# Two layers of attention on one core: the second layer's key and value weights split during the output projection, other accumulator banks for its first gate block, the first modulation ranked ahead of all, small loads issued by GpSimd

## Chip, cores and metric

The kernel runs on one core of one Trainium2 chip. Its time is device time in microseconds; the smaller the better. A profiled execution gives a trace; TensorE (PE in the rows), VectorE (DVE), ScalarE (ACT), GpSimd (POOL) and SyncE (SP, which here only issues loads and stores) each work through a queue of their own in order, and wait for each other by semaphores. The granted TensorE clock was 1.0 in the profiled execution.

## The reference

A trunk of two layers on 256 tokens of width 1024, in float32. Each layer makes a modulation from the condition `c` (shift, scale and gate), normalises `x`, modulates it, mixes tokens by attention and adds the gated result to `x`:

```python
cond = jax.nn.silu(c)
for i in range(DEPTH):
    shift, scale, gate = jnp.split(cond @ ada_w[i] + ada_b[i], 3, axis=-1)
    h = rms_norm(x, norm_g[i]) * (1 + scale[:, None, :]) + shift[:, None, :]
    y = nsa_mixer(h, ...) if i == 0 else moba_mixer(h, ...)
    x = x + gate[:, None, :] * y
```

Both mixers project `h` by a wide weight into queries (16 heads of 64), keys and values (4 heads) and a gate `z`, normalise queries and keys per head, rotate a quarter of each head by position, take softmax attention, multiply by `silu(z)` and project back by `w_out`. The first layer has three attentions side by side (over 15 compressed blocks, over selected blocks, over a window) and a gate for each. With 256 tokens every block is selected and the window covers all, so each is causal attention over all keys. The second layer has one block of 256 keys, so it is plain causal attention.

## The kernel before

The matrix products run in a reduced-width float format, each weight and activation split into a high part and the remainder (`hi`, `lo`); a product is three matmuls: hi·hi, hi·lo, lo·hi. A weight piece of 256 rows by 512 columns is loaded (`piece`), ScalarE casts it to `hi`, VectorE subtracts to get `lo` (`parts_of`, lines 624 to 631). Tokens come in two blocks of 128, called m = 0 and 1.

The program is first recorded and then ordered by a planner (`Plan`, from line 53). Each recorded operation has a cost from a table, its data dependencies, and a level: FIRST_OF_ALL -2, URGENT -1, CHAIN 0, FILL 1. `issue` walks a modelled clock per engine and gives each engine what can start first, then the lower level, then the earlier recorded one; an operation of a negative level that starts within 250 ns is waited for. So a change of a cost, a level or the order of recording can move any instruction of the whole kernel. Tiles come from tags with a fixed number of buffers: among them `hi` 4, `lo` 4, `raw` 5 (loaded pieces), `n_parts` 2, `qg` 5, and in the accumulator memory `acc` 2 and `ps` 6 banks. An operation whose tile finds no free buffer waits.

Stages that the change touches:

- **Start** (lines 487 to 1108). `c`, `x` and vectors are loaded; the first 128 columns of the modulation (`load_columns`, `ada_ss`) and the first 128 rows of the projection (`load_rows`) come first, so that the projection can begin on a part of the inner dimension; then the rest in stages (`START`). The modulation's result `AB` turns the normalised, transposed input into `HT`, the left operand of the projections. `small_loads` (lines 496 to 500) is a generator: six small loads (positions and five vectors), handed to SP one at a time between the big loads of `load_columns(1)` and `load_rows(1)`. Their reader on TensorE is the product of `ones` with `ROWV` in `tables` (line 1005), after which GpSimd computes rotation tables that are needed at the first key normalisation.
- **First layer's output projection and the next layer's entry** (lines 1364 to 1415). `out_products` runs the two token blocks one behind the other; when block 0 is done, its update of `x`, normalisation, modulation and split into `HT` (`x_part`, `next_h`) run at FIRST_OF_ALL while TensorE does block 1. Before block 1's last part, `first_parts` records the split of the first two of four key/value weight pieces of the second layer into the space of the first layer's keys (`KTF`), free by then. `chunk(m_in, KVB, ...)` then runs block 0 over all four pieces, then block 1.
- **Gate blocks** (`z_blocks`, lines 784 to 804). Each makes 512 columns of `z`, transposed, into two accumulator banks; tanh on ScalarE and a product on VectorE empty them into `zT`. In the second layer both blocks use the two `acc` banks, and their products are the filler beside the attention of `pair_b`.

Of the kernel before, what the change touches and what calls it, by code (L numbers as in the profile page):

```python
# [17 lines left out]
P = 128  # L18
# [34 lines left out]
class Plan:  # L53
# [120 lines left out]
    def _cost(self, engine, method, args, kw, aps):  # L174
        def free(a):
            n = 1
            for _, k in a.ap[1:]:
                n *= k
            return n

        if "dma" in method:
            self.bytes = free(aps[0]) * aps[0].shape[0] * 4
            if aps[1].shape[-1] <= 128 and self.bytes > 1e5:
                self.bytes *= SHORT_ROWS
            if self.bytes <= 1e5:
                self.bytes += SMALL
            return ISSUE if engine == "A" else max(ISSUE, self.bytes / RATE)
        psum = any(str(a.space).endswith("PSUM") for a in aps)
        n = max(free(a) for a in aps)
        if engine == "T":  # L190
            if method == "transpose":
                return 262.0 if aps[1].dtype == F32 else 180.0
            cols = free(aps[2])
            if aps[2].dtype == F32:
                m = free(aps[1])
                if "tile_position" in kw and m <= 64:
                    return max(cols * 4.28 * max(32, m) / P, 60.0)
                return 2 * max(cols * 2.14, 264.0)
            return max(cols * (1.07 if aps[2].dtype == F32R else 1.0), 264.0)
        if engine == "A":  # L200
            return 0.833 * n + (51.0 if psum else 94.0) + 93.0 * sum(isinstance(kw.get(k), bass.AP) for k in ("bias", "scale", "accum_out"))
        if engine == "G":
            return 1.5 * n + 270.0
        if method == "reciprocal":
            return 6.5 * n + 68.0
        fast = not psum and (method == "tensor_copy" or method.startswith("tensor_scalar"))
        pointers = len(aps) - 2 if method.startswith("tensor_scalar") else 0
        return (0.521 if fast else 1.042) * n + 68.0 + 61.0 * pointers
# [22 lines left out]
    def issue(self, opening=()):  # L231
# [51 lines left out]
        while done < len(ops):  # L283
# [57 lines left out]
            clock[e] = end  # L341
            seen = end + self.SEEN[e]
            if "bytes" in op:
                if e == "A":
                    seen = start + (BEHIND if op["level"] > 0 else 2400.0)
                else:
                    wire = max(wire, start + ISSUE + FIRST_BYTE) + op["bytes"] / (EARLY_RATE if start < 5e4 else RATE)
                    seen = wire + (450.0 if start < 5e4 else LANDED)
                    landings.append(seen)
                    if start < DEEP:  # L350
                        clock[e] = max(start + ISSUE, landings[-8] if len(landings) >= 8 else 0.0)
# [49 lines left out]
def kernel(  # L401
# [82 lines left out]
    def row(ap, n):  # L484
        return bass.AP(tensor=ap.tensor, offset=ap.offset, ap=[[n, 1], [1, n]])
# [7 lines left out]
        A.dma_start(R[ROW_B1 - 8:ROW_B1 - 8 + 4, :], rows_of(nsa_cmp_b1, 4))  # L493
        A.dma_start(R[ROW_PE - 8:ROW_PE - 8 + 32, :], rows_of(nsa_cmp_pe, 32))

    def small_loads():
        yield Q.dma_start(PR[:, 0].bitcast(I32), bass.AP(tensor=positions.tensor, offset=positions.offset, ap=[[P, 2], [1, P]]))
        for at, ap, n in ((0, nsa_q_norm, 64), (64, nsa_k_norm, 192), (256, moba_q_norm, 64), (320, moba_k_norm, 64),
                          (384, nsa_gate_b, 48)):
            yield Q.dma_start(ROWV[:, at:at + n], row(ap, n))  # L500

    identF = const.tile([P, P], F32, name="identF")
    make_identity(nc, identF)
# [277 lines left out]
            if count[m] == 8 // KP:  # L781
                done(m, accs[m])

    def z_blocks(w, c0, out):

        accs = [tile_of("acc", 2, S) for _ in range(2)]
        for kp in range(4):
            parts = parts_of(piece(w, kp, (c0, 512)))
            for k in range(KP):
                kt = KP * kp + k  # L790
                for b in range(4):
                    cols = slice(b * P, (b + 1) * P)
                    with plan.at(FILL):
                        for i, (a, part) in enumerate(((0, 0), (0, 1), (1, 0))):
                            T.matmul(accs[b // 2][:, b % 2], parts[part][:, k, cols], HT[:, a, kt, :],
                                     start=(kt == 0 and i == 0 and b % 2 == 0), stop=(kt == 7 and i == 2),
                                     skip_group_check=True)
            if kp < 3:
                yield
        for acc in accs:  # L800
            t, zT = tile_of("y", 2, S), tile_of("zT", 2, S)
            A.activation(t, acc, AF.Tanh, scale=0.5)
            V.scalar_tensor_tensor(zT, t, 1.0, acc, op0=OP.add, op1=OP.mult)
            out += [zT[:, 0], zT[:, 1]]
# [113 lines left out]

    loaded, kv_w = {}, {}

    smalls = small_loads()
    TABLES = 0
    R_AFTER = 0

# [12 lines left out]
    def load_columns(k):  # L937

        pieces = []
        for q in range(2):  # L940
            t = tile_of("early", 2, 4, P)
            pieces.append([t[:, 0], t[:, 1]])
            for s in range(2):
                with plan.at(CHAIN):
                    Q.dma_start(t[:, s], bass.AP(tensor=ada_w.tensor, offset=ada_w.offset + 4 * q * P * 3 * D + s * D + k * P,
                                                 ap=[[3 * D, P], [P * 3 * D, 4], [1, P]]))
                if k:
                    next(smalls, None)
        return pieces

    def load_rows(k):

        a, b = tile_of("early", 1024), tile_of("early", 768)
        rows = slice(k * P, (k + 1) * P)
        with plan.at(CHAIN):
            for c0 in (0, 512):
                Q.dma_start(a[:, c0:c0 + 512], w_in[rows, 1024 + c0:1536 + c0])
            if k:
                next(smalls, None)
            Q.dma_start(b[:, 0:512], w_in[rows, 2048:2560])  # L960
            if k:
                next(smalls, None)
            Q.dma_start(b[:, 512:768], w_in[rows, 0:256])
        return a, b

# [1 line left out]
    lead_s.append(load_columns(1))  # L967
    lead_w.append(load_rows(1))
    xT = [tile_of("n_out", 4, S) for _ in range(2)]
    xs, first_t = [], []  # L970
    RT1 = const.tile([P, ROW_ADA + 16], F32, name="RT1")
    for m in range(2):
        xm, ss = tile_of("n_in", D), tile_of("ss", 16)[:, 0:1]
        xs.append(xm)
        with plan.at(URGENT):
            A.activation(xm, X[:, m, :], AF.Square, accum_out=ss)
            r = rstd_of(ss, 1, 1.0 / D)
        for q in range(2):
            sl = slice(512 * q, 512 * q + 512)
            t = tile_of("ps", 4, P)  # L980
            with plan.at(FILL if q else URGENT):
                if q:
                    A.activation(xm[:, sl], X[:, m, sl], AF.Copy, scale=r)
                else:
                    V.tensor_scalar_mul(xm[:, sl], X[:, m, sl], r)
                with plan.group():
                    for k in range(4):
                        T.transpose(t[:, k, :], xm[:, (4 * q + k) * P:(4 * q + k + 1) * P], identF)
            with plan.at(FILL):
                A.copy(xT[q][:, 1 - q:, m * P:(m + 1) * P], t[:, 1 - q:])  # L990
            if not q:
                first_t.append(t)
        if m == R_AFTER:
            columns(R, 8)
            V.tensor_scalar_add(RT1[:, ROW_ADA + 8:ROW_ADA + 16], RT[:, ROW_ADA + 8:ROW_ADA + 16], 1.0)
# [60 lines left out]
                G.tensor_copy(TC[:, j, m, 0:16], TR[:, kind, m])  # L1056
        return TCS, NBc, TC, TR, TS

    def parts_2d(t, cuts):
        n = t.shape[1]  # L1060
        hi, lo = tile_of("hi", n), tile_of("lo", n)
        for c0, c1 in zip(cuts, cuts[1:] + (n,)):
            with plan.at(FILL):
                A.copy(hi[:, c0:c1], t[:, c0:c1])
                V.tensor_sub(lo[:, c0:c1], t[:, c0:c1], hi[:, c0:c1].bitcast(F32))
        return hi, lo

    for k in range(2):
        with plan.at(URGENT):
            at_once(ada_ss(0, k, 1, lead_s[k]))  # L1070
            for m in range(2):
                toks = slice(m * P, (m + 1) * P)
                src = xT[0][:, k, toks] if k else first_t[m][:, 0]
# [3 lines left out]
                    affine(h, src, 0, k, V)  # L1077
                    V.tensor_sub(HT[:, 1, k, toks], h, HT[:, 0, k, toks].bitcast(F32))
        a, b = lead_w[k]
        w = [(p, sl) for p, cuts in ((parts_2d(a, (0, 512) if not k else (0,)), (0, 512, 1024)), (parts_2d(b, (0,)), (0, 512, 768)))  # L1080
             for sl in (slice(c0, c1) for c0, c1 in zip(cuts, cuts[1:]))]
        for m in range(2):
            for ci, ((hi, lo), sl) in enumerate(w):
# [6 lines left out]
    for at, (what, k0, *rest) in enumerate(START):  # L1090
        load_stage(what, k0, *rest)
        if at == TABLES:
            at_once(smalls)
            TCS, NBc, TC, TR, TS = tables()
        if what == "s":
            nk = rest[0]
# [300 lines left out]
    at_hand = {}  # L1397

    def first_parts():
        for kp in range(2):  # L1400
            at_hand[kp] = parts_of(piece(m_in, kp, *KVB), (KTF[:, 2 * kp], KTF[:, 2 * kp + 1]))

    out_products(w_out, done_a, FINE, first_parts)
    assert not side
# [18 lines left out]
    make_q(raw_q, 4, QT, 2)  # L1423
    side.append(ada_gate(1))
    zT = []
    for c0 in (1536, 2048):
        for _ in z_blocks(m_in, c0, zT):
            beside()

    def pair_b(i):  # L1430
# [61 lines left out]
```

## Time and profile before

| | |
|---|---|
| median of 3 runs | 322.57 us (321.73 to 322.77) |
| profiled execution | 322.3 us, span 320.5 us |
| PE busy | 307.2 us, 96% |
| VectorE busy | 242.1 us, 76% |
| ScalarE busy | 204.9 us, 64% |
| GpSimd busy | 24.8 us, 8% |
| loaded from HBM | 64.36 MB, 204 GB/s over the span |

A timeline row reads: start, duration (us), engine, line, operation, output tile <- input tiles, shape, count of merged instructions, and in brackets the idle time of the engine before it with what ended that time. Nearly all instructions have line 373, where the planner issues them, so they are told apart by tiles. PEld is TensorE's weight load. The ends of matmuls are modelled and overlap the next start; the starts are what counts.

### The profile page before, as it was taken

To read this page: it belongs to the slowest core of one execution; us is meant where nothing else is said; L and a number is where in the kernel's file an instruction comes from. 1 tells how busy PE (TensorE), PEld (TensorE's weight loads), DVE (VectorE), ACT (ScalarE), POOL (GpSimd) and SP (SyncE) were. 2 spreads that over 40 slices of the span, in tenths; PEclk is the share of its full clock that TensorE was granted. 3 is DMA by queue.
4 is the path that set the end of the run, shared out by engine and by line. 5 is a ranking of instruction groups with operands and counts; after the bars stand their busy time and mean duration, and the time that the engine had idled before them with its cause. 6 is when DMAs were issued, how large, how long until landed. Compare 5 with 4: busy or idle time off the path is not lost.

```text
span 320.5 us, 6156 instructions
## 1 busy us (share of the span) xinstructions
PE 307.2 (96%) x2141; PEld 245.3 (77%) x2141; DVE 242.1 (76%) x732; ACT 204.9 (64%) x486; POOL 24.8 (8%) x96
## 2 busy tenths in 40 slices
PE   4899999999999999999999999988999989999995
PEld 4666677777757897768788888856888988886884
DVE  4764375669972999636979877893999999999564
ACT  5635145765735896465899854894676689988320
POOL 6038930000000000000000000000000000000000
PEclk9999999999999999999999999999999999999999
DMA  8999999559799805778074539236589651136302
GB/s 251 319 332 368 367 360 272 159 175 338 265 325 296 292 7 177 235 252 304 24 261 133 190 81 281 105 73 193 167 271 306 183 190 27 54 122 200 127 33 100
DMA packets 43995, 65.81 MB, mean 205 GB/s; under 512 B 4042, under 2 KB 20793, under 8 KB 43964
## 3 DMA queue, kind: packets, MB, share of 16 engines
q1 hardware_dynamic: 43796, 65.36, 63.1%
q8 instruction: 17, 0.28, 0.4%
q14 instruction: 14, 0.11, 0.1%
q10 hardware_dynamic: 168, 0.06, 0.1%
HBM read 64.36 MB, written 1.05 MB: 204 GB/s over the span
## 4 chain that ended last, share of the span: by engine, by line
PE 72%; DVE 12%; DMA 7%; ACT 4%; issue 3%; ACTq 0%; SPq 0%; DVEq 0%
PE ps L373 46%; PE acc L373 26%; DVE lo L373 3%; DVE rs L373 2%; DMA p<-in_nsa_cmp_w_dram 2%; DMA raw<-in_nsa_w_in_dram 2%; DMA y<-in_ada_b_dram 2%; ACT n_out L373 1%; DVE gate L373 1%; DVE n_out L373 1%; DMA early<-in_nsa_w_in_dram 1%; ACT hi L373 1%; ACT HT L373 1%; DVE p L373 1%; DVE ss L373 1%
## 5 line engine op out<-in xcount | busy, mean ns | idle before, releaser
L373 DVE TENSOR_TENSOR lo<-raw,hi 128x1024 fp32r<-128x1024 f32 (+1 forms) x50 | 58.9, 1184 | 21.3 <-ACT hi L373 21.1
L373 ACT CAST hi<-raw 128x1024 fp32r<-128x1024 f32 (+1 forms) x50 | 51.0, 1025 | 34.0 <-PE acc L373 19.7
L373 PE MATMUL acc<-hi,HT 128*128 128x512 f32 (+1 forms) x176 | 54.4, 381 | 2.0 <-ACT HT L373 1.5
L373 PE MATMUL acc<-HT,hi 128*128 128x256 f32 x256 | 49.8, 285 | 1.0 <-DVE zT L373 1.0
L373 ACT ACTIVATE p<-p,tiny 128x128 f32<-128x128 f32 (+1 forms) x96 | 42.9, 454 | 7.5 <-DVE tiny L373 7.4
L373 PEld LDWEIGHTS acc<-HT,hi 128*128 128x128 f32 x256 | 40.1, 188 | 1.8 <-DVE zT L373 1.2
L373 PEld LDWEIGHTS acc<-hi,HT 128*128 128x128 f32 x176 | 32.1, 188 | 10.5 <-issue 2.4
L373 PE MATMUL acc<-HT,lo 128*128 128x256 f32 x128 | 36.8, 288 | 0.0
L373 PE MATMUL acc<-lo,HT 128*128 128x512 f32 (+1 forms) x88 | 33.5, 383 | 1.5 <-DVE lo L373 1.5
L373 DVE CUSTOM_DVE_ANT_0 p<-ps,causal 128x128 f32<-128x128 f32 (+1 forms) x96 | 30.9, 346 | 3.3 <-PE ps L373 3.3
L373 PE MATMUL ps<-hi,HT 128*128 128x512 f32 (+1 forms) x96 | 28.2, 366 | 0.0
L373 PE MATMUL ps<-KTA,qg 128*128 128x256 f32 (+1 forms) x192 | 27.1, 286 | 0.0
L373 ACT COPY pT<-ps 128x384 f32<-128x384 f32 x48 | 21.7, 483 | 5.7 <-PE ps L373 5.6
L373 PEld LDWEIGHTS ps<-KTA,qg 128*128 128x128 f32 x192 | 24.1, 189 | 1.6 <-issue 1.4
L373 PEld LDWEIGHTS acc<-HT,lo 128*128 128x128 f32 x128 | 24.2, 189 | 0.3 <-issue 0.2
L373 PE MATMUL ps<-hi,qg 128*128 128x256 f32 (+1 forms) x96 | 23.7, 320 | 0.0
L373 PE MATMUL acc<-hi,qg 128*128 128x512 f32 x64 | 22.6, 403 | 0.0
L373 PE MATMUL ps<-identF,p 128*128 128x128 f32 x144 | 21.7, 277 | 0.0
L373 PEld LDWEIGHTS acc<-lo,HT 128*128 128x128 f32 x88 | 16.5, 188 | 5.2 <-DVE lo L373 2.8
L373 PEld LDWEIGHTS ps<-hi,HT 128*128 128x128 f32 x96 | 16.8, 188 | 4.5 <-issue 2.5
L373 PE MATMUL ps<-pT,VA 128*64 128x256 f32 (+1 forms) x192 | 19.1, 334 | 0.0
L373 PEld LDWEIGHTS ps<-identF,p 128*128 128x128 f32 x144 | 16.1, 141 | 3.5 <-issue 1.0
(199 smaller groups left out, 565.2 us busy)
## 6 DMA issues: line engine op xcount, KB each, us to landing
raw<-in_ada_w_dram SPq DMA_DIRECT2D x32, 512.0 KB, 4.4
raw<-in_moba_w_in_dram SPq DMA_DIRECT2D x20, 512.0 KB, 4.5
early<-in_ada_w_dram SPq DMA_DIRECT2D x12, 512.0 KB, 9.7
raw<-in_nsa_w_in_dram SPq DMA_DIRECT2D x12, 512.0 KB, 7.3
early<-in_nsa_w_in_dram SPq DMA_DIRECT2D x9, 512.0 KB
p<-in_nsa_cmp_w_dram SPq DMA_DIRECT2D x16, 256.0 KB, 3.7
raw<-in_nsa_w_out_dram SPq DMA_DIRECT2D x8, 512.0 KB, 6.0
raw<-in_moba_w_out_dram SPq DMA_DIRECT2D x8, 512.0 KB, 4.6
```

The source lines that it names most:

```text
L373: r = getattr(self.engines[e], method)(*[self._real(a) for a in args], **{k: self._real(a) for k, a in kw.items()})
```

## The change

Five edits.

1. `first_parts` splits all four key/value pieces of the second layer, the third into two `n_parts` buffers and the fourth into two `qg` buffers.
2. `z_blocks` takes the tag of its accumulators; the second layer's first gate block uses two `ps` banks, the second block `acc` as before.
3. The first modulation step (`ada_ss(0, 0, ...)`) goes from URGENT to FIRST_OF_ALL. The copies of the transposed input out of the accumulator memory, recorded before it until now, are recorded after it and made to depend on its last operation, as are the `lo` subtractions of the first projection piece.
4. The six small loads go from SP to GpSimd's queue, all at FILL level ahead of everything else; the generator and its calls are gone.
5. The planner's cost and landing model: only SP's loads are charged by bytes; a load by GpSimd costs its engine 450 ns and is taken as landed 5.5 us after issue at FILL level, as ScalarE's were.

```diff
@@ Plan._cost
-            return ISSUE if engine == "A" else max(ISSUE, self.bytes / RATE)
+            return max(ISSUE, self.bytes / RATE) if engine == "S" else ISSUE
@@ Plan.issue
-                if e == "A":
+                if e != "S":
                     seen = start + (BEHIND if op["level"] > 0 else 2400.0)
@@
-    def small_loads():
-        yield Q.dma_start(PR[:, 0].bitcast(I32), bass.AP(tensor=positions.tensor, ...))
+    with plan.at(FILL):
+        G.dma_start(PR[:, 0].bitcast(I32), bass.AP(tensor=positions.tensor, ...))
         for at, ap, n in ((0, nsa_q_norm, 64), (64, nsa_k_norm, 192), (256, moba_q_norm, 64), (320, moba_k_norm, 64),
                           (384, nsa_gate_b, 48)):
-            yield Q.dma_start(ROWV[:, at:at + n], row(ap, n))
+            G.dma_start(ROWV[:, at:at + n], row(ap, n))
@@ z_blocks
-    def z_blocks(w, c0, out):
-        accs = [tile_of("acc", 2, S) for _ in range(2)]
+    def z_blocks(w, c0, out, home="acc"):
+        accs = [tile_of(home, 2, S) for _ in range(2)]
@@ start
-            with plan.at(FILL):
-                A.copy(xT[q][:, 1 - q:, m * P:(m + 1) * P], t[:, 1 - q:])
+            evac.append((xT[q][:, 1 - q:, m * P:(m + 1) * P], t[:, 1 - q:]))
...
-    def parts_2d(t, cuts):
+    def parts_2d(t, cuts, after=()):
...
                 A.copy(hi[:, c0:c1], t[:, c0:c1])
-                V.tensor_sub(lo[:, c0:c1], t[:, c0:c1], hi[:, c0:c1].bitcast(F32))
+                with plan.group(after=after):
+                    V.tensor_sub(lo[:, c0:c1], t[:, c0:c1], hi[:, c0:c1].bitcast(F32))
...
     for k in range(2):
+        with plan.at(URGENT if k else FIRST_OF_ALL):
+            at_once(ada_ss(0, k, 1, lead_s[k]))
+        known = [plan.ops[-1]["id"]] if not k else ()
+        if not k:
+            for dst, src in evac:
+                with plan.at(FILL), plan.group(after=known):
+                    A.copy(dst, src)
         with plan.at(URGENT):
-            at_once(ada_ss(0, k, 1, lead_s[k]))
...
-        w = [... parts_2d(a, (0, 512) if not k else (0,)) ...]
+        w = [... parts_2d(a, (0, 512) if not k else (0,), known) ...]
@@ first_parts
-        for kp in range(2):
-            at_hand[kp] = parts_of(piece(m_in, kp, *KVB), (KTF[:, 2 * kp], KTF[:, 2 * kp + 1]))
+        homes = [(KTF[:, 0], KTF[:, 1]), (KTF[:, 2], KTF[:, 3]),
+                 (tile_of("n_parts", KP, 512), tile_of("n_parts", KP, 512)),
+                 (tile_of("qg", KP, 512), tile_of("qg", KP, 512))]
+        for kp in range(4):
+            at_hand[kp] = parts_of(piece(m_in, kp, *KVB), homes[kp])
@@ second layer
-    for c0 in (1536, 2048):
-        for _ in z_blocks(m_in, c0, zT):
+    for c0, home in ((1536, "ps"), (2048, "acc")):
+        for _ in z_blocks(m_in, c0, zT, home):
             beside()
```

More of the change, by code (lines that the diff above doesn't have):

```diff
@@ L494 @@
         A.dma_start(R[ROW_PE - 8:ROW_PE - 8 + 32, :], rows_of(nsa_cmp_pe, 32))
-    def small_loads():
-        yield Q.dma_start(PR[:, 0].bitcast(I32), bass.AP(tensor=positions.tensor, offset=positions.offset, ap=[[P, 2], [1, P]]))
+    with plan.at(FILL):
+        G.dma_start(PR[:, 0].bitcast(I32), bass.AP(tensor=positions.tensor, offset=positions.offset, ap=[[P, 2], [1, P]]))
         for at, ap, n in ((0, nsa_q_norm, 64), (64, nsa_k_norm, 192), (256, moba_q_norm, 64), (320, moba_k_norm, 64),
                           (384, nsa_gate_b, 48)):
-            yield Q.dma_start(ROWV[:, at:at + n], row(ap, n))
+            G.dma_start(ROWV[:, at:at + n], row(ap, n))
     identF = const.tile([P, P], F32, name="identF")
@@ L919 @@
     loaded, kv_w = {}, {}
-    smalls = small_loads()
     TABLES = 0
@@ L946, in load_columns @@
                                                  ap=[[3 * D, P], [P * 3 * D, 4], [1, P]]))
-                if k:
-                    next(smalls, None)
         return pieces
@@ L957, in load_rows @@
                 Q.dma_start(a[:, c0:c0 + 512], w_in[rows, 1024 + c0:1536 + c0])
-            if k:
-                next(smalls, None)
             Q.dma_start(b[:, 0:512], w_in[rows, 2048:2560])
-            if k:
-                next(smalls, None)
             Q.dma_start(b[:, 512:768], w_in[rows, 0:256])
@@ L969 @@
     xT = [tile_of("n_out", 4, S) for _ in range(2)]
-    xs, first_t = [], []
+    xs, first_t, evac = [], [], []
     RT1 = const.tile([P, ROW_ADA + 16], F32, name="RT1")
@@ L1079 @@
         a, b = lead_w[k]
-        w = [(p, sl) for p, cuts in ((parts_2d(a, (0, 512) if not k else (0,)), (0, 512, 1024)), (parts_2d(b, (0,)), (0, 512, 768)))
+        w = [(p, sl) for p, cuts in ((parts_2d(a, (0, 512) if not k else (0,), known), (0, 512, 1024)), (parts_2d(b, (0,)), (0, 512, 768)))
              for sl in (slice(c0, c1) for c0, c1 in zip(cuts, cuts[1:]))]
@@ L1092 @@
         if at == TABLES:
-            at_once(smalls)
             TCS, NBc, TC, TR, TS = tables()
```

## The prediction, made before the result

> **What bounds the kernel now.** I read the page first, then windows of the span, then timelines of the three places that the change touches.
>
> ```profile
> span 320.5 us, 6156 instructions
> PE 307.2 (96%) x2141; PEld 245.3 (77%) x2141; DVE 242.1 (76%) x732; ACT 204.9 (64%) x486; POOL 24.8 (8%) x96
> DMA  8999999559799805778074539236589651136302
> raw<-in_ada_w_dram SPq DMA_DIRECT2D x32, 512.0 KB, 4.4
> ```
>
> TensorE is busy 96% of the span, so all that the change can win is TensorE idle time. The DMA row says that the first seven slices, some 52 us, run at the full rate of the DMA engines. In windows (columns: window, length, busy us and count of PE, PEld, DVE, ACT, POOL, clock, DMA share, GB/s):
>
> ```profile
> 8.00:12.00 4.00, 3.65 (x49) 2.79 (x40) 3.10 (x13) 3.08 (x7) 0.00 (x0) 1.00 1.07 326
> 12.00:16.00 4.00, 3.16 (x27) 2.22 (x27) 2.94 (x7) 2.26 (x5) 0.00 (x0) 1.00 1.12 312
> ```
>
> ```profile
> 230.00:290.00 60.00, 59.03 (x454) 53.42 (x453) 59.32 (x190) 47.66 (x120) 0.00 (x0) 1.00 0.53 173
> ```
>
> So the start has two limits, TensorE and the DMA engines (share 1.07 and 1.12), and the second layer from 230 to 290 has two as well: PE 59.03 and VectorE 59.32 of 60. A gain on PE there counts only if DVE comes forward too.
>
> **Part 1, key and value weights split in the output projection.** Before, two of the four pieces are split ahead, into the free KTA tile; the other two wait for buffers of `hi` and `lo`. The second layer's entry on TensorE:
>
> ```profile
> 207.48 2.96 PE L373 MATMUL acc<-KTA,HT 128*128 128x512 f32 x12
> ...
> 210.28 0.39 PE L373 MATMUL acc<-hi,HT 128*128 128x512 f32 x1
> 211.25 0.51 PE L373 MATMUL acc<-lo,HT 128*128 128x512 f32 x1 [0.57 <-DVE lo L373]
> ...
> 212.29 0.85 PE L373 MATMUL acc<-hi,HT 128*128 128x512 f32 x3
> 213.60 1.39 PE L373 MATMUL ps<-identF,n_in 128*128 128x128 f32 x8 [0.45 <-DVE n_in L373]
> ...
> 215.76 0.40 PE L373 MATMUL acc<-hi,HT 128*128 128x512 f32 x1
> 216.82 0.50 PE L373 MATMUL acc<-lo,HT 128*128 128x512 f32 x1 [0.66 <-DVE lo L373]
> ...
> 217.85 0.63 PE L373 MATMUL acc<-hi,HT 128*128 128x512 f32 x2
> 218.82 3.06 PE L373 MATMUL acc<-KTA,HT 128*128 128x512 f32 x12 [0.35 <-ACT VA L373]
> ```
>
> The row x12 takes 2.96 with a last end of 0.39, so one such matmul streams (2.96 - 0.39) / 11 = 0.23 us. From start to start less 0.23, TensorE loses 211.25 - 210.28 - 0.23 = 0.74; then 213.60 - 212.29 - 3 x 0.23 = 0.62; then 216.82 - 215.76 - 0.23 = 0.83; then 218.82 - 217.85 - 2 x 0.23 = 0.51. Together 2.70. The first and third are waits for `lo` parts. The second waits for token block 1's normalisation, the fourth for ScalarE to empty the accumulator. What sets these, on DVE and ACT:
>
> ```profile
> 185.34 8.18 SPq L373 DMA_DIRECT2D raw<-in_moba_w_in_dram  x4
> 199.89 0.63 ACT L373 ACTIVATE y<-X 128x512 f32<-128x512 f32 x1 [2.99 <-DVE X L373]
> 201.02 0.42 DVE L373 TENSOR_TENSOR y<-ps,gate 128x256 f32<-128x256 f32 x1 [0.37 <-PE ps L373]
> 202.54 0.16 DVE L373 TENSOR_TENSOR ss<-ss 128x1 f32<-128x1 f32 x1 [0.56 <-ACT y L373]
> 203.74 1.05 ACT L373 CAST hi<-raw 128x1024 fp32r<-128x1024 f32 x1 [0.29 <-PE acc L373]
> 209.97 1.22 DVE L373 TENSOR_TENSOR lo<-raw,hi 128x1024 fp32r<-128x1024 f32 x1
> 213.46 1.22 DVE L373 TENSOR_TENSOR lo<-raw,hi 128x1024 fp32r<-128x1024 f32 x1
> 224.38 1.23 DVE L373 TENSOR_TENSOR lo<-raw,hi 128x1024 fp32r<-128x1024 f32 x1 [5.03 <-ACT hi L373]
> ```
>
> The cast at 203.74 waited for TensorE to release a `hi` buffer. With homes of their own (`n_parts`, `qg`) the two casts, 2 x 1.05, fit into ScalarE's 2.99 us before 199.89 and cost nothing, if the four pieces issued until 185.34 + 8.18 = 193.52 have landed (4.4 us for a load in the row quoted with the page, so near 198); without that gap they would cost 2.10 on the way to the next normalisation. The two `lo` subtractions, 2 x 1.22 = 2.44, find only 0.37 + 0.56 us of idle DVE before 202.54, and the planner gives an engine to whatever is ready when the urgent step is further off. I expect them in these two gaps, pushing block 0's update and normalisation back by (1.22 - 0.37) + (1.22 - 0.56) = 1.51 at most. Queued behind them on DVE is the chain that ends in HT, and TensorE waits for that at 207.48. Against this, the stalls of 0.74 and 0.83 go, and the pieces of the next chunk get `hi`/`lo` buffers sooner, so TensorE can run query products while it waits for block 1 (the 0.62 and 0.51). Best case: 2.70 - 0.62 = 2.08 gained. Worst case: 2.70 - 1.51 - 0.62 = 0.57 gained. I take **1.4**, near the middle, because the row at 207.48 starts only after work of the projection that covers part of a delay. VectorE follows: it idles 5.03 us before 224.38 for a `hi` buffer that TensorE frees, so its crowded stretch starts earlier by what TensorE gained, and the two subtractions are already behind it.
>
> **Part 2, `ps` banks for the first gate block.** The second block's first matmul waits for the first block's accumulators:
>
> ```profile
> 260.93 0.28 PE L373 MATMUL acc<-HT,hi 128*128 128x256 f32 x1
> 262.18 0.39 PE L373 MATMUL acc<-HT,hi 128*128 128x256 f32 x1 [0.97 <-DVE zT L373]
> ```
>
> ```profile
> 268.93 1.22 DVE L373 TENSOR_TENSOR lo<-raw,hi 128x1024 fp32r<-128x1024 f32 x1
> ```
>
> With separate banks the wait goes: 262.18 - 260.93 - 0.12 (rows of this shape start about 0.12 apart, half of 0.23) = 1.13. No instruction is added. Two of the six `ps` banks are held by the gate block, which leaves four for scores and transposes; the gate products are the filler that covers this. What is late next is DVE: once TensorE has done the products whose parts are ready, it needs what DVE makes next, the `lo` of 268.93 for one. If DVE has not come forward, the bubble only moves, gain 0. I take **0.9** of bounds 0 and 1.1, since DVE comes forward by part 1's 1.4.
>
> **Parts 3 and 4, the start.**
>
> ```profile
> 5.15 0.95 POOL L373 MEMSET gate<- 128x1024 f32 x1
> 9.16 0.41 SPq L373 DMA_DIRECT2D rs<-in_positions_dram  x1
> 10.07 0.29 DVE L373 COPY row<-ps 128x128 f32<-128x128 f32 x1 [0.49 <-PE ps L373]
> 11.62 0.63 ACT L373 CAST hi<-early 128x512 fp32r<-128x512 f32 x1
> 12.33 0.80 ACT L373 ACTIVATE HT<-ps,AB 128x128 fp32r<-128x128 f32 x2
> 12.84 0.50 PE L373 MATMUL acc<-hi,HT 128*128 128x512 f32 x1 [1.19 <-ACT HT L373]
> 14.86 0.24 SPq L373 DMA_DIRECT2D y<-in_nsa_gate_b_dram  x1
> 19.33 0.99 PE L373 MATMUL ps<-y,ones 1*128 1x432 f32 x2
> 29.56 0.73 PE L373 MATMUL acc<-hi,HT 128*128 128x512 f32 x2 [0.27 <-ACT HT L373]
> ```
>
> First modulation ahead of all: between the `row` copy (ends 10.36) and the first HT (12.33) stand transposes on PE, a `lo` subtraction on DVE and the cast 11.62 to 12.25 on ACT. Putting the copies and the subtraction behind the modulation shortens these 1.97 us. I estimate that 0.6 of them is queueing: 0.3 on ACT, whose cast ended at 12.25, just ahead of HT, and as much for the transposes and the subtraction. So 0.6 at the 12.84. The subtraction then comes some 1 us later and TensorE needs it one matmul on, so the lower bound is 0. TensorE is also stopped again at 29.56 for HT of the second modulation, whose weights arrive at the rate of full DMA engines; of the 0.6 only what this later wait does not take back remains.
>
> Small loads: six issues leave SP (the first, 0.41, at 9.16; the last, 0.24, at 14.86), so between 6 x 0.24 = 1.4 and 6 x 0.41 = 2.5 us of issue. The big loads go out earlier but not faster: in both windows the share is over 1. I count 0, and as upper bound the 0.27 that TensorE waits at 29.56 behind such loads. GpSimd issuing a load is nowhere in this trace. Its queue is free at 6.10. By the nearest rows an issue costs 0.24 (SP) to 0.95 (a GpSimd instruction), so the last is out between 7.5 and 11.8, sooner than the 14.86 of before, and the first reader on TensorE stood at 19.33. The planner charges 450 ns each and takes data as there 5.5 us after issue, so that with the memset first it will put the reader near 15.4. Both ends leave room; I count 0 for it.
>
> Parts 3 and 4 together: **0.4**, bounds 0 and 0.9 in this reading.
>
> **The sum.** The profiled execution took 322.3 (span 320.5 and 1.8 around it), 0.27 under the median 322.57 of three. 322.3 - 1.4 - 0.9 - 0.4 = 319.6, and with 0.27 added 319.9. All best: 322.57 - 2.08 - 1.13 - 0.9 = 318.5; all worst: 322.57 - 0.57 = 322.0.
>
> **Rivals.**
>
> *VectorE is the bound.* DVE is busy 59.32 of 60 from 230 to 290; if its start after the 5.03 us is not earlier (the new `hi` buffers are then full of the query chunk), TensorE only waits elsewhere. Then parts 1 and 2 give nothing after 230 and 0.4 remains, with some 0.3 for the work that DVE no longer has to do: 321.9. For it the full DVE; against it that what starts DVE at 224.38 is TensorE.
>
> *The split doesn't come earlier.* Normalisation steps are ranked ahead of splits; if no gap is offered, the two subtractions stay near 209.97 and 213.46 and only buffers change hands. Part 1 gives 0.2: 322.57 - 0.2 - 0.9 - 0.4 = 321.1.
>
> *Slower: GpSimd's loads come late and stop TensorE.* TensorE takes its queue in order; the reader of these rows is placed ahead of the projections, near 15.4. If GpSimd can issue only while DVE is idle, which is 4 - 3.10 and 4 - 2.94 of the two windows, about a quarter of the time, six issues of 0.41 take 2.5 / 0.25 = 10 us, until 16.1; with the 4.4 us to landing of the load row quoted with the page the reader starts at 20.5 and the stall is 5.1. It decides from a landing later than about 19: below that the parts above pay for it. Then 319.9 + 5.1 - 0.5 (the later wait before 29.56 takes some) = 324.5. Against it: the six move few bytes.
>
> The Trainium skill, SBUF — State Buffer, section SBUF: two separate sides, speaks for this rival: a load from GpSimd has its descriptors written by GpSimd, which is locked out while VectorE runs a two-port operation. In section A bandwidth-pool intuition that's wrong it gives about 3.1 us in place of 0.62 for one such load; six in a row would be 18.6 us, an estimate from that page, and 6.1 + 18.6 = 24.7 for the reader, by the same sum a time of 319.9 + 24.7 - 15.4 - 0.5 = 328.7. No row here shows such a load, so I give the rule no more than this rival's chance.
>
> **How the numbers follow.** Forecast 0.50 (319.9, own range 318.5 to 321.0); split not earlier 0.15 (321.1); VectorE bound 0.19 (321.9); GpSimd late 0.16 (324.5). The planner rewrites the order of the whole kernel, which I cannot price; I add about 0.7 on either side. The range is 317.8 to 323.6: below it lies little of the forecast, above it most of the last rival. A difference under 0.3%, 0.97 us, cannot be told from none, so faster means under 321.6, slower over 323.5. Faster: 0.50, most of the second case and a third of the third, 0.68. Slower: the last case, 0.15. Same: the rest, 0.17.
>
> **What would show it.** Part 1: four casts and subtractions into tiles other than `hi`/`lo` before 205, and 24 matmuls of the first key/value block without a wait for `lo`; a later start than 207.5 shows the 1.51. Part 2: no wait for zT between the two gate blocks; a new wait for `p` or `lo` soon after shows the bubble moved. Start: the first projection matmul near 12.2, and the second modulation's HT still near 29. The forecast is wrong if the matmul from `ones` waits for a load, if DVE's idle stretch before 224 stays at 5 us, or if block 0's normalisation slips by more than 1.5.

## The result, and the profile after

The changed kernel takes 318.71 us (median, 317.88 to 318.98) against 322.67 us: the ratio is 0.9884, 95% interval 0.9852 to 0.9917. In two further comparisons, told below, it was 0.9882 and 0.9865. The prediction said 319.9 us, range 317.8 to 323.6; the gain is 3.96 us where its terms added up to 2.7. The profiled execution took 318.98 us, its span is 317.3 us.

From the page of the changed kernel (span, busy times, and the queue that was not there before):

```profile
span 317.3 us, 6173 instructions
...
PE 307.2 (97%) x2141; PEld 245.2 (77%) x2141; DVE 241.6 (76%) x732; ACT 205.2 (65%) x486; POOL 26.5 (8%) x102
...
q0 software_dynamic: 192, 0.00, 0.0%
```

TensorE's busy time is that of before to a tenth: only idle time went. GpSimd has six instructions more, the loads.

**The second layer's entry.** Timelines of the changed kernel, TensorE first:

```profile
205.85 0.40 PE L373 MATMUL ps<-lo,qg 128*128 128x512 f32 x1
206.41 0.44 PE L373 MATMUL ps<-identF,n_in 128*128 128x128 f32 x2 [0.16 <-ACT n_in L373]
206.61 0.47 PE L373 MATMUL ps<-hi,qg 128*128 128x512 f32 x1
207.17 0.44 PE L373 MATMUL ps<-identF,n_in 128*128 128x128 f32 x2
207.46 0.73 PE L373 MATMUL acc<-KTA,HT 128*128 128x512 f32 x2
...
210.93 1.55 PE L373 MATMUL acc<-n_parts,HT 128*128 128x512 f32 x6
212.32 1.56 PE L373 MATMUL acc<-qg,HT 128*128 128x512 f32 x6
```

```profile
196.56 1.04 ACT L373 CAST n_parts<-raw 128x1024 fp32r<-128x1024 f32 x1
197.83 1.05 ACT L373 CAST qg<-raw 128x1024 fp32r<-128x1024 f32 x1 [0.22 <-DMA raw<-in_moba_w_in_dram]
...
204.90 1.05 ACT L373 CAST hi<-raw 128x1024 fp32r<-128x1024 f32 x1 [0.35 <-PE ps L373]
205.85 0.50 ACT L373 ACTIVATE n_in<-X,rs 128x256 f32<-128x256 f32 x1
```

```profile
201.65 1.22 DVE L373 TENSOR_TENSOR n_parts<-raw,n_parts 128x1024 fp32r<-128x1024 f32 x1
202.79 0.15 DVE L373 TENSOR_TENSOR ss<-ss 128x1 f32<-128x1 f32 x1
...
209.86 1.22 DVE L373 TENSOR_TENSOR qg<-raw,qg 128x1024 fp32r<-128x1024 f32 x1
...
225.30 0.69 DVE L373 TENSOR_REDUCE ss<-n_out 128x8 f32<-128x512 f32 x1 [4.60 <-ACT n_out L373]
```

The third and fourth pieces are read from `n_parts` and `qg`, and no row of TensorE from 200 to 226 us waits for `lo` any more; the four stalls, 2.70 us, are gone. New are two of 206.41 - 205.85 - 0.23 = 0.33 and 207.17 - 206.61 - 0.23 = 0.33: ScalarE's cast of a query piece at 204.90 stands ahead of the scaling of block 0 (205.85). Only one of the two subtractions got in ahead of the normalisation's sum `ss`; the other came at 209.86.

**The gate blocks.** TensorE in the changed kernel:

```profile
254.22 0.28 PE L373 MATMUL ps<-HT,hi 128*128 128x256 f32 x1
254.33 0.28 PE L373 MATMUL acc<-HT,hi 128*128 128x256 f32 x1
...
256.60 0.28 PE L373 MATMUL acc<-HT,hi 128*128 128x256 f32 x1
257.04 1.56 PE L373 MATMUL ps<-identR,n_parts 128*128 128x128 f32 x16 [0.17 <-DVE n_parts L373]
```

The second block follows the first by 0.11 us; of the 1.13 us stall there is left 257.04 - 256.60 - 0.12 = 0.32, a wait for VectorE.

**The start.** GpSimd, TensorE's reader of the small rows, ScalarE and the first projection matmul, and a window that spans the six issues (columns as in the prediction's windows), all of the changed kernel:

```profile
6.06 0.77 POOL L373 DMA_DIRECT2D rs<-in_positions_dram  x1
6.84 0.53 POOL L373 DMA_DIRECT2D y<-in_nsa_q_norm_dram  x1
...
8.78 0.48 POOL L373 DMA_DIRECT2D y<-in_nsa_gate_b_dram  x1
```

```profile
6.06:9.26 3.20, 3.20 (x28) 2.59 (x27) 2.92 (x16) 1.39 (x4) 3.20 (x7) 1.00 1.14 301
```

```profile
12.80 0.50 PE L373 MATMUL acc<-hi,HT 128*128 128x512 f32 x1 [0.68 <-ACT HT L373]
...
18.23 0.28 PE L373 MATMUL ps<-hi,HT 128*128 128x256 f32 x1
18.44 0.99 PE L373 MATMUL ps<-y,ones 1*128 1x432 f32 x2
```

```profile
11.77 0.62 ACT L373 CAST hi<-early 128x512 fp32r<-128x512 f32 x1 [0.32 <-DMA early<-in_nsa_w_in_dram]
12.29 0.80 ACT L373 ACTIVATE HT<-ps,AB 128x128 fp32r<-128x128 f32 x2
```

The reader stands at 18.44 and waits for no load: the six had landed 3.3 to 5.3 us after their issue, the last near 14.1. The first projection matmul starts at 12.80, in this profile as in that of before (12.84): `HT` is queued on ScalarE behind a cast that had itself waited for its load. But TensorE's idle time ahead of it is 0.68 us where the prediction's row has 1.19; more profiles are compared below.

### The profile page after: what moved, and what is told of

It reads as the page before. It is cut to its first block, busy times and chain, and to the rows that moved or that the text cites. A ratio compares the mean times of both kernels' runs of the same rounds, so it can differ in the third digit from the quotient of the medians.

```text
span 317.3 us, 6173 instructions
## 1 busy us (share of the span) xinstructions
PE 307.2 (97%) x2141; PEld 245.2 (77%) x2141; DVE 241.6 (76%) x732; ACT 205.2 (65%) x486; POOL 26.5 (8%) x102
## 4 chain that ended last, share of the span: by engine, by line
PE 82%; DVE 7%; DMA 5%; ACT 3%; issue 2%; ACTq 0%; SPq 0%; DVEq 0%
PE ps L373 49%; PE acc L373 33%; DVE lo L373 3%; ACT hi L373 2%; DMA raw<-in_ada_w_dram 2%; DMA y<-in_ada_b_dram 2%; DMA early<-in_nsa_w_in_dram 1%; DVE n_out L373 1%; DVE gate L373 1%; DVE rs L373 0%; ACT n_in L373 0%; DVE p L373 0%; DVE ss L373 0%; DVE zT L373 0%; ACT p L373 0%
## 5 line engine op out<-in xcount | busy, mean ns | idle before, releaser
L373 DVE TENSOR_TENSOR lo<-raw,hi 128x1024 fp32r<-128x1024 f32 (+1 forms) x48 | 56.4, 1181 | 11.0 <-ACT hi L373 10.8
L373 ACT CAST hi<-raw 128x1024 fp32r<-128x1024 f32 (+1 forms) x48 | 48.9, 1022 | 23.1 <-DMA raw<-in_nsa_w_in_dram 8.3
L373 PE MATMUL acc<-hi,HT 128*128 128x512 f32 (+1 forms) x160 | 49.6, 381 | 1.5 <-ACT n_in L373 0.8
L373 PE MATMUL acc<-HT,hi 128*128 128x256 f32 x192 | 37.7, 285 | 0.0
L373 PEld LDWEIGHTS acc<-hi,HT 128*128 128x128 f32 x160 | 29.0, 188 | 9.8 <-issue 2.9
L373 PEld LDWEIGHTS acc<-HT,hi 128*128 128x128 f32 x192 | 30.1, 188 | 0.6 <-issue 0.6
L373 PE MATMUL acc<-lo,HT 128*128 128x512 f32 (+1 forms) x80 | 30.3, 380 | 0.2 <-DVE lo L373 0.2
L373 PE MATMUL acc<-HT,lo 128*128 128x256 f32 x96 | 27.7, 289 | 0.0
L373 ACT ACTIVATION_READ_ACCUMULATOR p<-p,tiny 128x1 f32 x96 | 18.8, 196 | 0.0
L373 DVE TENSOR_SCALAR p<-p,tiny 128x256 f32<-128x256 f32 (+1 forms) x64 | 18.1, 329 | 0.0
```

The costliest lines, as they stand in the source:

```text
L373: r = getattr(self.engines[e], method)(*[self._real(a) for a in args], **{k: self._real(a) for k, a in kw.items()})
```

## Experiments

One reading is used for all of them. The start of one matmul, the first of the first layer's output projection into an `acc` bank, is taken as a mark, since what follows it is nearly free of loads that come late. In the kernel before and in the changed one (TensorE's timeline, with its head line):

```profile
core 0 of [0], span 320.5 us
...
184.11 0.50 PE L373 MATMUL acc<-hi,qg 128*128 128x512 f32 x1
```

```profile
core 0 of [0], span 317.3 us
...
183.87 0.50 PE L373 MATMUL acc<-hi,qg 128*128 128x512 f32 x1
```

From the mark to the end of the span it is 320.5 - 184.11 = 136.39 us before and 317.3 - 183.87 = 133.43 us after, so 2.96 us lie behind the mark. Mark and span are those of the one profiled execution of each kernel, the median that of all its runs. All kernels:

| kernel | mark, us | span, us | mark to end, us | median, us | ratio to before (95%) |
|---|---|---|---|---|---|
| before | 184.11 | 320.5 | 136.39 | | |
| changed kernel | 183.87 | 317.3 | 133.43 | 318.71 | 0.9884 (0.9852 to 0.9917) |
| split alone | 184.07 | 318.8 | 134.73 | 320.17 | 0.9929 (0.9904 to 0.9954) |
| banks alone | 184.91 | 321.7 | 136.79 | 321.84 | 0.9978 (0.9953 to 1.0002) |
| split and banks | 184.15 | 317.8 | 133.65 | 318.86 | 0.9877 (0.9839 to 0.9914) |
| both edits of the start | 183.28 | 319.6 | 136.32 | 321.25 | 0.9958 (0.9934 to 0.9981) |
| modulation alone | 185.68 | 322.1 | 136.42 | 323.89 | 1.0042 (1.0020 to 1.0064) |
| small loads alone | 182.80 | 319.1 | 136.30 | 321.16 | 0.9971 (0.9943 to 0.9998) |
| changed kernel, second time | 183.09 | 316.5 | 133.41 | 318.32 | 0.9882 (0.9847 to 0.9916) |
| changed, subtractions later | 183.37 | 319.2 | 135.83 | 320.42 | 0.9942 (0.9919 to 0.9964) |
| changed kernel, third time | 182.94 | 316.3 | 133.36 | 318.03 | 0.9865 (0.9841 to 0.9888) |
| changed without modulation's edit | 184.24 | 317.3 | 133.06 | 317.95 | 0.9854 (0.9830 to 0.9879) |
| changed, rank only | 182.14 | 315.2 | 133.06 | 317.59 | 0.9845 (0.9824 to 0.9867) |
| changed, hold only | 183.06 | 316.3 | 133.24 | 318.05 | 0.9862 (0.9839 to 0.9884) |

The result and the four experiments from modulation alone to subtractions later ran beside a kernel before of 322.67 us, the four ahead of these beside one of 322.25, the last four beside one of 322.59. Kernels with the same edits in the second layer agree behind the mark to 0.12 us with none of them (136.30 to 136.42) and to 0.59 with both (133.06 to 133.65).

### The split alone

The kernel before with `first_parts` of the change:

```diff
-        for kp in range(2):
-            at_hand[kp] = parts_of(piece(m_in, kp, *KVB), (KTF[:, 2 * kp], KTF[:, 2 * kp + 1]))
+        homes = [(KTF[:, 0], KTF[:, 1]), (KTF[:, 2], KTF[:, 3]),
+                 (tile_of("n_parts", KP, 512), tile_of("n_parts", KP, 512)),
+                 (tile_of("qg", KP, 512), tile_of("qg", KP, 512))]
+        for kp in range(4):
+            at_hand[kp] = parts_of(piece(m_in, kp, *KVB), homes[kp])
```

> The kernel before with part 1 alone (all four key/value pieces split into buffers of their own). Theory (each place pays by itself): the four stalls at the second layer's entry, 2.70 us in the trace before, shrink as in the changed kernel, where TensorE lost about 2.2 us less between 200 and 220 us; the wait for zT between the two gate blocks (0.97 us idle) stays. 322.6 - 2.2 = 320.4 us. Rival, VectorE is the bound from 230 to 290 us: what the entry gains is lost again before the end, 322.0 us or more. Rival, the start carries the gain: 322.5 us.

Measured: 320.17 us, ratio 0.9929. TensorE's timeline of this kernel between the gate blocks:

```profile
254.46 0.28 PE L373 MATMUL acc<-HT,hi 128*128 128x256 f32 x1
256.07 0.38 PE L373 MATMUL acc<-HT,hi 128*128 128x256 f32 x1 [1.34 <-DVE zT L373]
```

Behind the mark the split gains 136.39 - 134.73 = 1.66 us. That is the 2.70 us of stalls, less the two new ones of 0.33 (here at 206.61 and 207.37), less 0.36 by which the wait between the gate blocks grew (256.07 - 254.46 - 0.12 = 1.49 where it was 1.13): 1.68. VectorE is not the bound here: what the entry gains stays gained, but for this 0.36.

That the buffers carry it, and not the place in the program, shows without a run: with the last two splits recorded in `chunk` again, but into the same buffers of their own, the planner puts every instruction of the engines at the same place as in the changed kernel.

### The banks alone

The kernel before with `home="ps"` for the first gate block, nothing else:

```diff
-    for c0 in (1536, 2048):
-        for _ in z_blocks(m_in, c0, zT):
+    for c0, home in ((1536, "ps"), (2048, "acc")):
+        for _ in z_blocks(m_in, c0, zT, home):
...
```

> The kernel before with part 2 alone (first gate block in ps banks). Theory of the prediction: the wait of 0.97 us for zT goes, but VectorE has not come forward, so TensorE stops soon after for p, n_parts or lo instead; the time stays within 0.4 us of 322.6, and the first gap after the gate blocks is new. Rival: the wait was a plain loss and its removal is worth 1.1 us by itself, 321.5 us. Rival: fewer ps banks for scores cost more than the wait, above 323.0 us.

Measured: 321.84 us, ratio 0.9978, an interval that holds both nothing and half a per cent. The profiled execution took 323.32 us and is the slowest of the twelve, so its span does not stand for the kernel; but what happened in it can be followed. TensorE and ScalarE in it, then TensorE before:

```profile
293.30 0.82 PE L373 MATMUL ps<-identF,p 128*128 128x128 f32 x6
...
295.01 0.40 PE L373 MATMUL ps<-hi,qg 128*128 128x512 f32 x1
296.38 1.25 PE L373 MATMUL ps<-pT,VA 128*64 128x256 f32 x8 [0.97 <-ACT pT L373]
```

```profile
293.80 1.05 ACT L373 CAST hi<-raw 128x1024 fp32r<-128x1024 f32 x1 [2.17 <-DMA raw<-in_moba_w_out_dram]
```

```profile
293.72 0.82 PE L373 MATMUL ps<-identF,p 128*128 128x128 f32 x6
```

Mark to end is 136.79 us, 0.40 more than before. But the bubble did not move, as the prediction said it would without the split. The wait for `zT` is gone, and the transposes of `p`, the same count of matmuls behind the mark in both kernels, start 293.30 - 184.91 = 108.39 us behind it where it was 293.72 - 184.11 = 109.61: 31 us after the gate blocks TensorE is still 1.22 us ahead, with VectorE as full as before (busy 59.12 of the 60 us from 230 to 290). All of it is lost in one stop of 296.38 - 295.01 - 0.23 = 1.14 and the rows around it. That stop is ScalarE's: its cast waited 2.17 us for a weight load, and `pT` is queued behind it. The trace has 16 landings for this load; 15 are in by 292.02, the last at 293.78. Measured from the mark, the load was issued as before (102.44 against 102.33 us) and was whole 1.14 us later (108.87 against 107.73). Whether another execution has this late part was not tested. The timed runs give the banks alone some 0.7 us (0 to 1.5), so the rival that the wait was a plain loss of 1.1 us is not excluded.

### Split and banks together

> The kernel before with parts 1 and 2, the start as before. Theory: 2.2 at the entry and 1.1 at the gate blocks, 322.6 - 3.3 = 319.3 us, nearly all of the gain of the whole change (318.7 us). Rival, the start's edits bring 0.4 or more: 319.3 us is missed and the time lies at 319.8 us or above. If the planner's order of the whole kernel is what moved, the time can be anywhere from 318 to 322 us and the gaps at the two places will not explain it.

Measured: 318.86 us, ratio 0.9877. Mark to end is 133.65: the banks gain 134.73 - 133.65 = 1.08 on top of the split. Together the two give 2.74 of the 2.96 us behind the mark; the 0.22 left is less than the 0.59 by which kernels with both edits differ there. The median lies 0.44 under the 319.3 expected.

### Both edits of the start

> The kernel before with the start's edits alone (first modulation ahead of all, small loads by GpSimd). Theory from the changed kernel's trace: the first projection matmul starts at 12.8 us as before, and work at 138, 168 and 185 us starts 0.2 us earlier; 322.4 us. The prediction's term: 0.4 us, 322.2 us. Rival, the start is worth most of the gain: 320 us or less. The entry stalls (2.7 us) and the zT wait stay as before in each.

Measured: 321.25 us, ratio 0.9958, so 0.6 to 2.1 us faster: more than the 0.2 that I had read from one profile of each kernel, and above the prediction's 0.4. Behind the mark nothing changes (136.32 against 136.39), so it lies in the first layer. The next two runs part it.

### Modulation alone, small loads alone

The kernel before with edit 3 of the change alone, and with edits 4 and 5 alone (the hunks shown with the change).

> The kernel before with the first modulation ahead of all, alone (small loads still issued by SP). Seen so far: with both edits of the start the time was 1.0 us less (interval 0.6 to 2.1), though in single profiles the first projection matmul stands at 12.80 and 13.26 us with them and at 12.84 to 13.32 us without. Theory: the modulation's edit brings nothing by itself (time within 0.4 us of before, the idle time ahead of the first projection matmul near 1.1 us minus what the transposes fill, its start at 12.8 to 13.3). Rival, as the prediction put it: it is the modulation that pays, 0.4 us or more, with that start half a microsecond earlier than 12.8.

> The kernel before with the small loads on GpSimd's queue, alone. The prediction counted 0. Theory now: with SP free of six issues of 0.24 to 0.41 us (1.4 to 2.5 us in all) the big loads of the start go out earlier, and this is where the start's 1.0 us comes from: 321.5 us or less, and the matmul from ones stands near 18.5 us in place of 19.3 to 19.8. Rival: loads at the full rate of the DMA engines can't be had earlier, 322.3 us. Rival, GpSimd late: the matmul from ones waits for a load, above 323 us.

Measured: the modulation's edit alone makes the kernel slower, 323.89 us, ratio 1.0042 (0.6 to 2.1 us). The small loads alone make it faster, 321.16 us, ratio 0.9971. The prediction had it the other way round.

What the small loads do is seen in the view of DMA queues from 8 to 30 us, of the kernel before and of the kernel with the small loads alone (packets, bytes moved, mean rate):

```profile
DMA packets 7238, 7.46 MB, mean 339 GB/s; under 512 B 353, under 2 KB 5699, under 8 KB 7235
```

```profile
DMA packets 7636, 7.70 MB, mean 350 GB/s; under 512 B 540, under 2 KB 6097, under 8 KB 7633
```

With the six issues gone from SP the DMA engines move more in the same 22 us. Over all profiles taken here it is 7.24 to 7.51 MB, mean 7.34, in the five kernels whose small loads are SP's, and 7.48 to 7.70, mean 7.66, in nine with them on GpSimd. The difference, 0.32 MB at 340 GB/s, is 0.9 us, and the ratio gives 0.0029 x 322.67 = 0.9 (interval 0.1 to 1.8). TensorE's third group of modulation products (`ps<-early,condz`) starts at 23.25 to 23.90 in the five and at 22.02 to 22.96 in the nine. So the DMA shares of 1.07 and 1.12 did not mean that no more could be moved. SP issues the big loads in the same order with and without this edit, but the planner also put some of TensorE's matmuls up to 62 us in another order, and no run parts the two.

Why the modulation's edit alone costs is seen at the second modulation. VectorE and TensorE of that kernel:

```profile
29.67 0.23 DVE L373 TENSOR_TENSOR AB<-ps,RT 128x2 f32<-128x2 f32 x2 [5.30 <-ACT hi L373]
```

```profile
28.55 0.61 PE L373 MATMUL ps<-selP,row 128*128 128x2 f32 x4
...
29.21 0.28 PE L373 MATMUL ps<-hi,HT 128*128 128x256 f32 x1
30.72 0.74 PE L373 MATMUL acc<-hi,HT 128*128 128x512 f32 x2 [1.23 <-ACT HT L373]
```

The same two rows of `AB` and of the product that it reads, before:

```profile
28.48 0.22 DVE L373 TENSOR_TENSOR AB<-ps,RT 128x2 f32<-128x2 f32 x2 [4.80 <-PE ps L373]
```

```profile
27.76 0.61 PE L373 MATMUL ps<-selP,row 128*128 128x2 f32 x4
```

TensorE stops 1.23 us for `HT`, 0.27 before. Two things add up. `AB` starts 29.67 - 28.55 = 1.12 us behind the product that it reads, 28.48 - 27.76 = 0.72 before. And the planner left TensorE less to do meanwhile: the last matmul ahead of the stop starts 29.21 - 28.55 = 0.66 us behind that product; before, it started at 29.02, 1.26 us behind it. The profile puts the wait of `AB` down to ScalarE's cast of a weight piece. That is inferred from times; `AB` reads nothing of the cast, and in the program it waits for that product and for the copy of `row` before it, in this kernel as in the one before. What holds it 0.4 us longer is not known.

In the changed kernel (VectorE, then TensorE) `AB` is as late behind the product, 1.13 us, but TensorE has matmuls to do until 29.52, and no row there waits for `HT`:

```profile
28.47 0.23 DVE L373 TENSOR_TENSOR AB<-ps,RT 128x2 f32<-128x2 f32 x2 [5.05 <-ACT hi L373]
```

```profile
27.34 0.61 PE L373 MATMUL ps<-selP,row 128*128 128x2 f32 x4
...
29.52 0.74 PE L373 MATMUL acc<-hi,HT 128*128 128x512 f32 x2
```

### The changed kernel again

> The changed kernel itself, once more beside the others on one chip. Theory that the parts add (split 2.1, banks on top of it 1.1, start 0.4 to 1.0): 318.3 us, and a second profile of it, to tell what differs between two executions of the same order: start of the first projection matmul and the waits for loads near 97 and 105 us differ by some tenths; the intervals behind 205 us do not. If the parts don't add: 319 us.

Measured: 318.32 us, ratio 0.9882; third time 318.03. These steps add: by medians 2.1 for the split, 1.3 more with the banks and 1.0 for the start make 4.4, and 322.67 - 4.4 = 318.3. The three profiles differ at the mark by 0.93 us (182.94 to 183.87) and behind it by 0.07.

### The subtractions later

The changed kernel, with the third and fourth piece's subtractions bound to the end of block 0's normalisation:

```diff
+        ready = [plan.ops[-1]["id"]]
         for kp in range(4):
-            at_hand[kp] = parts_of(piece(m_in, kp, *KVB), homes[kp])
+            at_hand[kp] = parts_of(piece(m_in, kp, *KVB), homes[kp], ready if kp > 1 else ())
@@ parts_of
...
-            V.tensor_sub(lo, t, hi.bitcast(F32))
+            with plan.group(after=after):
+                V.tensor_sub(lo, t, hi.bitcast(F32))
```

> The changed kernel, in which the third and fourth piece's lo subtractions on VectorE may start only after the last split of token block 0's normalisation (they come some 5 us later; the casts stay early). The prediction charged the early subtractions up to 1.51 us on block 0's normalisation. Prediction's reading: without them TensorE starts block 0's key/value products up to 1.5 us earlier against the work before them, gain up to 1 us if the lo parts still come in time (needed some 3.5 and 5 us after that start). Rival: the early subtraction costs the normalisation only the 0.25 us by which the ss addition moved in the changed kernel, so the time stays within 0.3 us of the changed kernel's; a loss, if TensorE now waits for the lo of n_parts or qg.

Measured: 320.42 us, ratio 0.9942: 2.1 us slower than the changed kernel beside it. TensorE's timeline:

```profile
204.44 1.32 PE L373 MATMUL ps<-identF,n_in 128*128 128x128 f32 x8
...
210.52 0.50 PE L373 MATMUL acc<-lo,HT 128*128 128x512 f32 x1 [0.35 <-DVE lo L373]
...
216.10 1.43 PE L373 MATMUL acc<-qg,HT 128*128 128x512 f32 x5 [0.42 <-DVE qg L373]
218.35 0.50 PE L373 MATMUL acc<-lo,HT 128*128 128x512 f32 x1 [0.83 <-DVE lo L373]
```

Block 0's transposes start 204.44 - 183.37 = 21.07 us behind the mark, as in the kernel before (205.18 against 184.11, 21.07); in the changed kernel it is 21.52 to 21.53 in its three profiles. So the early subtraction costs the normalisation 0.46 us, and putting it off gives just that back. But VectorE then does both subtractions between block 1's steps, and TensorE's waits for `lo` and for `qg` are back. Mark to end grows by 135.83 - 133.41 = 2.42. What came is the loss named last.

### Without the modulation's edit

> The changed kernel without the modulation's edit (split, banks and GpSimd's small loads stay). Theory from the single edits: split and banks 3.3, small loads 0.9, sum 4.2 of 322.6: 318.4 us; and since the modulation's edit cost 1.4 us by itself, this kernel should be faster than the changed one by 0.5 to 1.4 us, 317.0 to 317.8 us, with VectorE's AB of the second modulation released by TensorE (as with the small loads alone) and not by ScalarE's hi cast, and no stop of TensorE for HT or lo near 29.5. Rival: the loss of the modulation's edit occurs only while SP still issues the small loads; then this kernel equals the changed one within 0.4 us, 318.3 us.

Measured: 317.95 us, ratio 0.9854, beside 318.03 for the changed kernel: no difference that can be told. The rival holds: the modulation's edit costs only while SP issues the small loads. `AB` is here put down to TensorE, as expected, 0.71 us behind its product, but there was no stop left to save.

### Rank only, hold only

```diff
@@ rank only
-        known = [plan.ops[-1]["id"]] if not k else ()
+        known = ()
...
@@ hold only
-        with plan.at(URGENT if k else FIRST_OF_ALL):
+        with plan.at(URGENT):
```

> The changed kernel with the first modulation at the level ahead of all, but the copies of the transposed input and the lo subtractions of the first piece not held back behind it. Theory A, holding back costs: AB of the second modulation is again released by TensorE and the time is 0.5 us or more under the changed kernel's 318.3. Theory B, the rank costs: as the changed kernel, 318.3 us, AB released by ScalarE's hi cast near 28 us.

> The changed kernel with the copies and the lo subtractions held back behind the first modulation, which keeps its old level. Theory A, holding back costs: as the changed kernel or slower, 318.3 us, AB of the second modulation released by ScalarE's hi cast. Theory B, the rank costs: 0.5 us or more faster than the changed kernel, under 317.8 us.

> The changed kernel once more, as the partner of the other three on one chip: 318.3 to 318.7 us, ratio to the kernel before 0.988. It tells whether the kernel without the modulation's edit is faster than it by more than the scatter of some 0.5 us.

Measured: 317.59, 318.05 and 318.03 us; the ratios' intervals overlap. Both theories fall: `AB` is put down to TensorE in either kernel, 0.71 us behind its product, so it takes the rank and the holding back together to make it late. All six profiles of kernels with both have it at 1.12 to 1.14 us, the eight others at 0.71 to 0.72. What does that was not found. Rank only has the lowest median of all, 0.44 under the changed kernel, which this measurement does not tell from none. Its profile shows what holding back had done to the first modulation (ScalarE, then TensorE, of rank only):

```profile
11.29 0.81 ACT L373 ACTIVATE HT<-ps,AB 128x128 fp32r<-128x128 f32 x2
...
12.83 0.65 ACT L373 CAST hi<-early 128x512 fp32r<-128x512 f32 x1
```

```profile
11.80 0.50 PE L373 MATMUL acc<-hi,HT 128*128 128x512 f32 x1
```

Here the second cast stands behind `HT`, and the first projection matmul starts at 11.80. In the changed kernel the copies are held back, and the planner put both casts ahead of `HT`. In two of its three profiles, the one shown among them, the second cast waits for its load and `HT` starts behind it (12.29 and 11.82); in the other the casts are done and `HT` waits for VectorE (12.18).

## Why the prediction was right, and where it was not

**The whole.** The time, 318.71, lies in the range and 1.2 us under the forecast: of the 3.96 us gained, the terms had 2.7. Of the 1.26 us missing 0.6 are the start's, 0.26 part 1's and 0.18 part 2's; the 0.22 left is not told from scatter. The total came out better than its reasons: part 2's condition and two steps of the start did not hold.

**Part 1**, forecast 1.4 of 0.57 to 2.08, measured 1.66 behind the mark (split alone). The mechanism held in its main steps: the casts fitted ScalarE's gap (196.56 and 197.83), the stalls for `lo` went, query products fill the wait for block 1. The term mis-sized is the delay of the normalisation, 1.51 at most for two subtractions: only one was put there, and it delayed the transposes by 0.46 and the first key and value product by 0.22 (23.59 us behind the mark against 23.37). Not foreseen: ScalarE's cast ahead of `n_in`, 2 x 0.33. My sign for VectorE was badly chosen: its idle stretch is nearly as long as before (4.60 us), but it ends in work of the key normalisation and not in a split that is late.

**Part 2**, forecast 0.9, measured 1.08 on top of the split. The size held, the condition did not: "If DVE has not come forward, the bubble only moves, gain 0". With the banks alone DVE had not come forward, and TensorE was still 1.22 us ahead 31 us later, far past the `lo` of 268.93 at which the bubble was to come back; what took it back in that one profile was a late load. By how much the banks gain alone stays open: 0 to 1.5 us.

**Parts 3 and 4**, forecast 0.4, measured 1.0 by medians (0.6 to 2.1 by the ratio). Here two steps failed, and the part came out at more than twice its forecast. "The big loads go out earlier but not faster: in both windows the share is over 1. I count 0" was wrong: they went faster, by 0.32 MB in 22 us, worth about 0.9 us. (The DMA row had been read in the same way, as a full rate; its first seven slices of 8.01 us are also 56 us and not 52.) The 0.6 of queueing ahead of the first modulation was there, but nothing of it lasted. TensorE's idle time ahead of the first projection matmul is 0.50 to 0.68 us in the six kernels with the whole of this edit and 1.04 to 1.19 in the six without any of it; that matmul starts at 12.76 in the mean against 13.24. By the third group of modulation products the gain is gone: with the small loads on GpSimd it starts at 22.53 in the mean with the edit and at 22.59 without, and the kernel without the edit is as fast. The prediction had counted only what a later wait does not take back; that wait took all. And when this edit stood alone, "the second modulation's HT" took more: a loss of 1.4 us, of which 1.23 - 0.27 = 0.96 are seen at that stop. That it costs nothing in the changed kernel is due to the small loads' edit.

**The rivals.** VectorE as the bound would have left the split alone at 322.0 or above; it ran at 320.17. The split did come earlier. GpSimd's loads took 0.48 to 0.77 us each to issue and were all out by 9.26 us, with VectorE busy 2.92 of the 3.20 us; the reader at 18.44 did not wait. In the Trainium skill, SBUF — State Buffer, section A bandwidth-pool intuition that's wrong, such a load takes 3.1 us beside a VectorE operation that holds the shared port. No load here took that long to issue, and the landings, 3.3 to 5.3 us after the issue, came while the big loads ran too. Whether one of VectorE's operations in that stretch holds the port is not shown by the trace, so the rule itself was not tested.

**The sum's baseline** was sound: 136.39 us behind the mark before, and the four kernels with the second layer unchanged (before, both start edits, modulation, small loads) lie within 136.30 to 136.42.

## What to carry to other kernels

Where the weights' splits are late at a stage's entry, look for buffers that are free there, and do the splits before the stage, even if that delays the urgent chain a little: here by 0.46 us, for 2.4 us gained against putting two of the subtractions off. Before a loss is read from one profile, see where its execution stands among the timed runs, and follow the stop to its end: the banks' loss of 0.40 was one late load in the slowest of twelve. Small loads between the big ones on one issuing queue cost some 0.9 us at the start here, though the DMA engines looked full. Put two edits of a stage to the test apart and together: the modulation's edit cost 1.4 us alone and nothing beside the small loads'.

## What was not expected of the hardware

Kernels with the same order of instructions on TensorE in the first layer reach the mark at very different times: before, split alone, banks alone, and split and banks at 184.07 to 184.91; small loads alone and the changed kernel without the modulation's edit at 182.80 and 184.24, a difference of 1.44 us. Behind the mark they agree better, to 0.12 us with the second layer unchanged. In that pair the scatter goes with the loads: 7.70 MB moved from 8 to 30 us, and 7.48, the least of the nine. A single profile therefore said little on the start; the timed runs and the interval from a mark said more, and even that interval held one late load in the banks' kernel.
